# RWKV scans: one set of operand tiles for all products of a step, pairwise products on halves of the rows, and the inverses' last transposes moved behind the state

## The chip, the cores and the metric

The kernel runs on one core of a Trainium2 chip. The metric is the device time of one execution in microseconds (us). The core's engines run their own instruction queues in order and wait for each other by semaphores: TensorE (PE; its weight loads are shown apart as PEld), VectorE (DVE), ScalarE (ACT), GpSimd (POOL), and SyncE (SP), which here issues DMA transfers.

## The reference, cut to what matters

One encoder layer on 1024 tokens of width 1024: windowed attention, a bidirectional RWKV-7 time mixing, gates, then an MLP and a gated embedding. The change touches the RWKV scan, one forward and one backward over 8 heads of 64:

```python
def step(state, inp):
    r_t, w_t, k_t, v_t, a_t, b_t = inp
    sa = jnp.einsum('dbhij,dbhj->dbhi', state, a_t)
    state = (state * w_t[..., None, :] + sa[..., :, None] * b_t[..., None, :]
             + v_t[..., :, None] * k_t[..., None, :])
    y = jnp.einsum('dbhij,dbhj->dbhi', state, r_t)
    return state, y
...
y = ys[0] + jnp.flip(ys[1], axis=1)
```

## The kernel before

The kernel computes the scan in 16 steps of 64 tokens (s = 0 to 15), both directions d = 0, 1 in each step. Earlier it has written, per direction and chunk, two operands to DRAM: `ra_d` (for each of four head pairs j a [128 rows, 128 columns] block; rows are the two heads' 64 channels, columns the 64 tokens of a and the 64 of r, already decayed inside the chunk) and `bk_d` (the same layout for b and k). From them a step makes

- the pairwise products of all tokens of a chunk (`products`, into PSUM tiles `gps`, masked by VectorE into `gm`). One full-array matmul makes both heads of a pair: the stationary operand is `bkp` with both heads' rows, and the moving one is `rm`, a tile in which the other head's rows are zero. `rm` and `bkp` are loaded for `products` alone, one step ahead;
- the chunk's keys transposed (`operands`, tile `tm`, from another copy of bk, `bkc`), and ra scaled on ScalarE by the decay of the chunk before (`rac`, a second copy of ra, loaded by `load_step` at the start of the step before it is used);
- w (`wps`, copied to `Wt`), u (`ups`: the chunk's inverse `zi` times `Wt`, copied into `UV`), the state's addition (`sps`, then `Tc`, the state `Sb` and its decayed copy `Sc`), and the output (`yps`, into `y`).

The inverse of a chunk's triangular matrix is taken for four chunks at once, once every four steps: `low` products (`lps`, copied to `lt` and `Lc`), then on VectorE a transpose `Lp`, 62 small multiplies and adds into `Z` (`tmp`, `Z`), and two transposes `Zn` and `Zt` of 1024 columns; `end_inverse` makes the off-diagonal blocks with TensorE (`qps`) at the end of the fourth step.

TensorE's order in the scan is written out by hand: `gap(i)` puts `FILL[i]` filler matmuls (gates `gmm`, then the attention's up-projection `uaps`) between the stages of a step. The helper `mmo` (its matmuls all show line L209) keeps that order. The other engines' order and SP's come from the scheduler, by priority. PSUM tiles named `gps`, `tmps`, `lps`, `qps` and `mups` share two buffers.

Of the kernel before, what the change touches and what calls it, by code (L numbers as in the profile page):

```python
# [17 lines left out]
P = 128  # L18
# [120 lines left out]
def block_kernel(ctx: ExitStack, tc: tile.TileContext, I: dict, out: bass.AP):  # L139
# [638 lines left out]
    def inverse(pl, lt):  # L778

        Lc = pl.tile([P, 32, 32], F32, name="Lc", tag="inv", bufs=3)  # L780
        for r0 in range(0, P, 32):
            k = r0 // 32 % 2
            nc.scalar.copy(Lc[r0:r0 + 32], lt[r0:r0 + 32, :, 32 * k:32 * k + 32])
        Lp = pl.tile([P, 32, 32], F32, name="Lp", tag="inv", bufs=3)
        nc.vector.transpose(out=Lp, in_=Lc.rearrange("s p t -> s t p"))
        Z = pl.tile([P, 32, 32], F32, name="Z", tag="inv", bufs=3)
        nc.gpsimd.memset(Z, 0.0)
        nc.gpsimd.memset(Z.rearrange("p r c -> p (r c)")[:, ::33], 1.0)
        tmp = pl.tile([P, 256], F32, name="tmp", bufs=1)
        for t in range(31):  # L790
            n, m = 31 - t, t + 1
            tv = tmp[:, 0:n * m].rearrange("p (n m) -> p n m", m=m)
            nc.vector.tensor_tensor(
                out=tv, in0=Lp[:, t + 1:32, t:t + 1].broadcast_to([P, n, m]),
                in1=Z[:, t:t + 1, 0:m].broadcast_to([P, n, m]), op=ALU.mult)
            nc.vector.tensor_tensor(out=Z[:, t + 1:32, 0:m], in0=Z[:, t + 1:32, 0:m], in1=tv, op=ALU.add)
        Zn = pl.tile([P, 32, 32], F32, name="Zn", tag="inv", bufs=3)
        Zt = pl.tile([P, 32, 32], F32, name="Zt", tag="inv", bufs=3)
        nc.vector.transpose(out=Zn.rearrange("r p c -> r c p"), in_=Z.rearrange("p r c -> p c r"))
        nc.vector.transpose(out=Zt.rearrange("c p r -> c r p"), in_=Z)  # L800
        return Zn, Zt
# [32 lines left out]
    rms = [BP.tile([P, 2, NP, P], F32, name=f"rm{i}") for i in range(2)]  # L834
    for t_ in rms:
        nc.gpsimd.memset(t_, 0.0)
    prods = {}

    def load_products(s, d):

        c = chunk(s, d)
        for q in range(2):
            nc.sync.dma_start(rms[d][own[q], q], ra_d[d, c][own[q]])
        b_ = BP.tile([P, NP, P], F32, name="bkp", bufs=2)
        nc.sync.dma_start(b_, bk_d[d, c])
        prods[s, d] = b_

    lts, zzs, lows = {}, {}, {}
    with ExitStack() as s2:
# [16 lines left out]
        for n in range(NT):  # L866
# [49 lines left out]
            if n == LOW_AT:  # L916
                lts[0] = list(low0)[-1]
                for d in range(ND):
                    load_products(0, d)
            if n == INV_AT:  # L920
                zzs[0] = inverse(BI, lts[0])
# [144 lines left out]
    ch_ra, ch_bk, ch_tm, ch_uv, Sc = {}, {}, {}, {}, {}  # L1066
# [4 lines left out]
    def products(s, d):  # L1071

        b_ = prods.pop((s, d))
        for h in range(2):
            ps = ps_gps([P, 2, 2, P], "gps")
            for j in range(2):
                mmo(ps[:, j], b_[:, 2 * h + j, :], rms[d][:, :, 2 * h + j, :], start=True, stop=True)
            nc.vector.tensor_tensor(  # L1078
                out=gm[d][:, s % NB, 4 * h:4 * h + 4, :], in0=ps.rearrange("p j q t -> p (j q) t"),
                in1=gmask[:, d, :].unsqueeze(1).broadcast_to([P, 4, P]), op=ALU.mult)  # L1080
        if s + 1 < NCH:
            load_products(s + 1, d)

    def load_step(s):

        UV = B.tile([P, ND, NH, 64], F32, name="UV", bufs=2)
        for d in range(ND):
            c = chunk(s, d)
            b_ = B.tile([P, NP, P], F32, name="bkc", bufs=2)
            nc.sync.dma_start(b_, bk_d[d, c])  # L1090
            r_ = B.tile([P, NP, P], F32, name="rac", bufs=4)
            nc.sync.dma_start(r_, ra_d[d, c])
            nc.sync.dma_start(UV[oth[d], d], v_d[c * C:(c + 1) * C, :].rearrange("t (h i) -> t h i", i=64))
            nc.gpsimd.memset(UV[own[d], d], 0.0)
            ch_ra[s, d], ch_bk[s, d] = r_, b_
        ch_uv[s] = UV

    def operands(s):

        for d in range(ND):  # L1100
            tp = ps_gps([P, NP, P], "tmps")
            for q in range(NP):
                tc.keep_in_program_order(nc.tensor.transpose(tp[:, q, :], ch_bk[s, d][:, q, :], ident))
            t_ = B.tile([P, NH, 64], F32, name="tm", bufs=4)
            nc.scalar.copy(t_, tp.rearrange("p q (h j) -> p (q h) j", h=2))  # L1105
            ch_tm[s, d] = t_
        for d in range(ND):
            if s > 0:
                for j in range(NP):
                    r_ = ch_ra[s, d][:, j, :]  # L1110
                    nc.scalar.activation(out=r_, in_=r_, func=AF.Copy, scale=Dt[:, d, j, s - 1:s])
# [11 lines left out]
    def wb_part(s, wp):  # L1123

        if s > 0:
            for q in range(NP):
                for d in range(ND):
                    mmo(wp[own[d], 2 * q:2 * q + 2, :], ch_ra[s, d][:, q, 0:64], Sb[1 - s % 2][:, d, q, :, :],
                        start=False, stop=True, skip_group_check=True)
# [3 lines left out]
    def u_part(s):  # L1133
# [6 lines left out]
        nc.scalar.copy(UV[own[1], 1], up[own[1]])  # L1140

    def s_part(s):
# [11 lines left out]
        if s < NCH - 2:  # L1154
            Sc[s] = B.tile([P, ND, NP, 64], F32, name="Sc")
            nc.vector.tensor_tensor(out=Sc[s], in0=Tc, in1=Dt[:, :, :, s].unsqueeze(3).broadcast_to([P, ND, NP, 64]), op=ALU.mult)

    def y_part(s):
        yp = PB.tile([P, ND, NP, C], F32, name="yps", bufs=1)
        for d in range(ND):  # L1160
            for q in range(NP):
                os = [yp[own[e], d, q, :] for e in range(2)]
                if s > 0:
                    for e in range(2):
                        mmo(os[e], Sb[1 - s % 2][:, d, q, e, :], ch_ra[s, d][:, q, 64:128], start=True, stop=False)
# [22 lines left out]
    load_step(0)  # L1188
# [19 lines left out]
    for s in range(NCH):  # L1208
# [23 lines left out]
        if nxt:  # L1232
            load_step(s + 1)
# [4 lines left out]
        gap(2)  # L1238
        if more:
# [5 lines left out]
        y_part(s)  # L1245
        wp = wa_part(s + 1) if nxt else None
# [613 lines left out]
```

## Time and profile before

| | |
|---|---|
| median of three runs | 1809.24 us (1803.22 to 1815.18) |
| profiled execution | 1803.17 us |
| its span, first to last instruction | 1801.4 us |
| mean granted TensorE clock | 0.983 |
| TensorE busy | 1702.8 us, 95% |
| VectorE busy | 1147.4 us, 64% |
| ScalarE busy | 882.0 us, 49% |
| products in the scan | first at 511 us, last at 832 us |

The busy share is an average over stages with different limits. A row of a timeline gives the start, the duration, the engine, the line, the operation, the output and inputs, and in square brackets the idle time before it with what ended that. Durations of matmuls overlap, so how long a stage holds TensorE is read from the starts of what stands ahead of it and behind it. float32 matmuls show two records each.

### The profile page before, as it was taken

What the parts mean: (1) busy time and instruction counts of PE and PEld (TensorE: products, weight loads), DVE (VectorE), ACT (ScalarE), POOL (GpSimd) and SP (SyncE); (2) the same over time, 40 slices, a digit from 0 to 9 for tenths busy, and PEclk for the clock granted to TensorE, in tenths of its full rate; (3) what the DMA queues carried; (4) which work ended last, traced back from release to release, by engine and by line L of the source; (5) the groups of instructions that cost most, each with busy time, mean ns of one, the idle gap of its engine ahead of it and who ended that gap; (6) DMA issues with size and microseconds to landing.
All of it is one profiled execution on the core that took longest, in us unless ns stands there. A gap on an engine that the chain in (4) does not pass through costs nothing. (4 is left out here: it accounts for less than half of the span.)

```text
span 1801.4 us, 29643 instructions
## 1 busy us (share of the span) xinstructions
PE 1702.8 (95%) x11288; PEld 1367.5 (76%) x11288; DVE 1147.4 (64%) x1955; ACT 882.0 (49%) x1624; POOL 279.0 (15%) x241
## 2 busy tenths in 40 slices
PE   7999998899999898989889989999999999999998
PEld 7987675666677777867568867888888888888887
DVE  5667887345936556676564387767666877685432
ACT  5546775357754555456632255444444444554221
POOL 3343223331232121111232000000000000000000
PEclk9999999999999999999999999999999999999999
DMA  5353446574377474576565305454456983674111
GB/s 199 96 136 120 145 144 198 159 198 116 102 205 204 132 201 142 172 204 206 176 218 179 106 36 164 158 164 141 150 166 224 324 258 114 191 222 134 60 41 47
DMA packets 281998, 285.96 MB, mean 159 GB/s; under 512 B 49408, under 2 KB 195712, under 8 KB 281728
## 3 DMA queue, kind: packets, MB, share of 16 engines
q1 hardware_dynamic: 273600, 270.76, 48.9%
q0 software_dynamic: 7824, 12.59, 2.5%
q8 instruction: 89, 1.46, 0.3%
q10 hardware_dynamic: 432, 0.73, 0.1%
q14 instruction: 53, 0.43, 0.1%
HBM read 203.26 MB, written 80.74 MB: 158 GB/s over the span
## 5 line engine op out<-in xcount | busy, mean ns | idle before, releaser
L1742 PE MATMUL ff2ps<-th,sl 128*128 128x512 f32 x448 | 174.3, 389 | 0.0
L1742 PE MATMUL ff2ps<-tl,sh 128*128 128x512 f32 x448 | 174.3, 389 | 0.0
L1742 PE MATMUL ff2ps<-th,sh 128*128 128x512 f32 x448 | 173.9, 389 | 0.0
L189 POOL TENSOR_TENSOR wlo<-wst,whi 128x512 fp32r<-128x512 f32 x76 | 104.6, 1389 | 269.2 <-ACT whi L188 223.6
L176 POOL TENSOR_TENSOR rstd<-ms,neghalf 128x1 f32<-128x1 f32 x24 | 13.2, 552 | 791.3 <-DVE ms L174 791.3
L188 ACT CAST sh<-sst 128x512 fp32r<-128x512 f32 x109 | 67.7, 622 | 99.9 <-PE ff2ps L1742 51.3
L189 DVE TENSOR_TENSOR sl<-sst,sh 128x512 fp32r<-128x512 f32 x109 | 75.0, 688 | 47.5 <-ACT sh L188 47.3
L1742 PEld LDWEIGHTS ff2ps<-th,sh 128*128 128x128 f32 x448 | 84.0, 188 | 17.9 <-ACT th L188 0.3
L1742 PEld LDWEIGHTS ff2ps<-tl,sh 128*128 128x128 f32 x448 | 84.1, 188 | 17.6
L1742 PEld LDWEIGHTS ff2ps<-th,sl 128*128 128x128 f32 x448 | 84.1, 188 | 17.3
L188 ACT CAST whi<-wst 128x512 fp32r<-128x512 f32 x100 | 60.4, 617 | 60.8 <-DMA wst<-in_w_in_dram 22.9
L188 ACT CAST w1h<-w1st 128x512 fp32r<-128x512 f32 x48 | 28.4, 620 | 100.1 <-DMA w1st<-in_w_ff_dram 66.6
L189 DVE TENSOR_TENSOR w1l<-w1st,w1h 128x512 fp32r<-128x512 f32 x48 | 31.8, 687 | 54.5 <-ACT w1h L188 54.5
L209 PE MATMUL gps<-rm,bkp 128*128 128x256 f32 x256 | 62.4, 386 | 1.6 <-ACT tm L1105 0.9
L1078 DVE TENSOR_TENSOR gm<-gps,gmask 128x512 f32<-128x512 f32 x64 | 43.8, 688 | 29.6 <-PE gps L209 29.6
L219 PE MATMUL mm<-hh,wlo 128*128 128x512 f32 x144 | 58.4, 406 | 2.5 <-DVE wlo L189 2.5
L215 PE MATMUL gmm<-hh,whi 128*128 128x512 f32 x144 | 58.9, 409 | 1.6 <-ACT whi L188 1.4
L219 PE MATMUL gmm<-hh,wlo 128*128 128x512 f32 x144 | 59.3, 412 | 1.1 <-POOL wlo L189 1.1
L215 PE MATMUL mm<-hh,whi 128*128 128x512 f32 x144 | 58.6, 407 | 1.7 <-ACT whi L188 1.7
L217 PE MATMUL gmm<-hl,whi 128*128 128x512 f32 x144 | 58.7, 408 | 0.0
L217 PE MATMUL mm<-hl,whi 128*128 128x512 f32 x144 | 57.9, 402 | 0.0
L209 PEld LDWEIGHTS gps<-rm,bkp 128*128 128x128 f32 x256 | 47.2, 189 | 11.3 <-ACT tm L1105 2.1
(410 smaller groups left out, 4975.2 us busy)
## 6 DMA issues: line engine op xcount, KB each, us to landing
wst<-in_w_in_dram SPq DMA_DIRECT2D x92, 256.0 KB, 3.6
tst<-in_w_ff_dram SPq DMA_DIRECT2D x80, 256.0 KB, 3.9
w1st<-in_w_ff_dram SPq DMA_DIRECT2D x32, 512.0 KB, 5.4
hid_S<-h SPq DMA_DIRECT2D x64, 256.0 KB, 2.1
sst<-hid_S SPq DMA_DIRECT2D x64, 256.0 KB, 3.1
hid_A<-h SPq DMA_DIRECT2D x48, 256.0 KB, 2.0
sst<-hid_A SPq DMA_DIRECT2D x45, 256.0 KB, 3.5
ra_d<-ra SPq DMA_DIRECT2D x8, 1024.0 KB, 4.6
```

The lines of the kernel that those rows point to most:

```text
L176: nc.gpsimd.tensor_tensor(out=r, in0=ms, in1=neghalf.broadcast_to([P, width]), op=ALU.pow)
L188: a = nc.scalar.copy(hi, src)
L189: b = (lo_eng or nc.vector).tensor_tensor(out=lo, in0=src, in1=hi.bitcast(F32), op=ALU.subtract)
L209: tc.keep_in_program_order(nc.tensor.matmul(*a, **kw))
L215: mm(ps, ah, bh, start=(i == 0), stop=False)
L217: mm(ps, ah, bl, start=False, stop=False)
L219: mm(ps, al, bh, start=False, stop=(i == n - 1))
L1078: nc.vector.tensor_tensor(out=gm[d][:, s % NB, 4 * h:4 * h + 4, :], in0=ps.rearrange("p j q t -> p (j q) t"), in1=gmask[:, d, :].unsqueeze ...
L1742: nc.tensor.matmul(banks[bs][i], x_[:, isl], y_, start=fresh and p + j == 0, stop=p == NPR - 1 and j == 2, skip_group_check=True)
```

## The change

1. `products` takes row halves. For each head pair it issues two matmuls, one per head, on 64 rows each (rows 0 to 63 and 64 to 127), with 128 stationary and 128 moving columns, each into a PSUM tile of its own. The zero-padded `rm` tiles and their memsets go. Each of the two masks on VectorE comes after all eight matmuls.
2. ra and bk are loaded once per step and direction into tiles that products, transposes and state products share: four rotating tiles for ra, three for bk. The loads of step s + 1 are issued behind `products(s)`, which is called two steps ahead of use. Steps 1 and 2 are loaded at the start. `load_step` becomes `load_v`, which loads only v.
3. The scaling of ra on ScalarE (`decayed`) is called after `u_part` of the step before, not with the transposes.
4. The inverse's two last transposes (`inverse_turned`) are called behind `y_part` of the fourth step and held on VectorE behind the last operation of the state (`Sc`).

```diff
+    def inverse_turned(pl, Z, behind=None):
         Zn = pl.tile([P, 32, 32], F32, name="Zn", tag="inv", bufs=3)
         Zt = pl.tile([P, 32, 32], F32, name="Zt", tag="inv", bufs=3)
-        nc.vector.transpose(out=Zn.rearrange("r p c -> r c p"), in_=Z.rearrange("p r c -> p c r"))
-        nc.vector.transpose(out=Zt.rearrange("c p r -> c r p"), in_=Z)
+        a = nc.vector.transpose(out=Zn.rearrange("r p c -> r c p"), in_=Z.rearrange("p r c -> p c r"))
+        b = nc.vector.transpose(out=Zt.rearrange("c p r -> c r p"), in_=Z)
+        if behind:
+            after(a, behind)
+            after(b, a)
         return Zn, Zt
...
+    NRA, NBK = 4, 3
+    def load_ra(s, d):
+        nc.sync.dma_start(ra_t[s % NRA, d], ra_d[d, chunk(s, d)])
+    def load_bk(s, d):
+        nc.sync.dma_start(bk_t[s % NBK, d], bk_d[d, chunk(s, d)])
...
     def products(s, d):
-        b_ = prods.pop((s, d))
-        for h in range(2):
-            ps = ps_gps([P, 2, 2, P], "gps")
-            for j in range(2):
-                mmo(ps[:, j], b_[:, 2 * h + j, :], rms[d][:, :, 2 * h + j, :], start=True, stop=True)
+        b_, r_ = bk_t[s % NBK, d], ra_t[s % NRA, d]
+        pss = [ps_gps([P, NP, P], "gps") for _ in range(2)]
+        for j in range(NP):
+            for q in range(2):
+                mmo(pss[q][:, j], b_[own[q], j, :], r_[own[q], j, :], start=True, stop=True)
+        for q in range(2):
             nc.vector.tensor_tensor(
-                out=gm[d][:, s % NB, 4 * h:4 * h + 4, :], in0=ps.rearrange("p j q t -> p (j q) t"),
-                in1=gmask[:, d, :].unsqueeze(1).broadcast_to([P, 4, P]), op=ALU.mult)
-        if s + 1 < NCH:
-            load_products(s + 1, d)
+                out=gm[d][:, s % NB, q::2, :], in0=pss[q],
+                in1=gmask[:, d, :].unsqueeze(1).broadcast_to([P, NP, P]), op=ALU.mult)
+        if 1 < s < NCH - 1:
+            load_ra(s + 1, d)
+            load_bk(s + 1, d)
...
         u_part(s)
         gap(2)
+        if nxt:
+            decayed(s + 1)
...
         y_part(s)
+        if s % NB == NB - 1 and s // NB < 3:
+            b = s // NB + 1
+            zzs[b] = inverse_turned(BI, zzs[b], state[0])
```

VectorE at the end of the first inverse that runs inside the scan (step 3). Before, from the last operations of the chain on:

```order
L793 TENSOR_TENSOR tmp<-Lp,Z 128x31
L796 TENSOR_TENSOR Z<-Z,tmp 128x31
L799 STREAM_TRANSPOSE Zn<-Z 128x32x32
L800 STREAM_TRANSPOSE Zt<-Z 128x32x32
L1139 COPY UV<-ups 64x512
L1078 TENSOR_TENSOR gm_4655<-gps,gmask 128x512 x2
L1150 TENSOR_TENSOR Tc<-sps,Sc 128x512
L1153 COPY Sb_4657<-Tc 64x8x64
L1156 TENSOR_TENSOR Sc<-Tc,Dt 128x512
L1130 COPY Wt<-wps 64x512
```

The same place in the change, from the copy of UV on (the chain's last operations stand directly ahead of it):

```order
L1151 COPY UV<-ups 64x512
L1092 TENSOR_TENSOR gm_4653<-gps,gmask 128x4x128 x2
L1165 TENSOR_TENSOR Tc<-sps,Sc 128x512
L1168 COPY Sb_4655<-Tc 64x8x64
L1171 TENSOR_TENSOR Sc<-Tc,Dt 128x512
L803 STREAM_TRANSPOSE Zn<-Z 128x32x32
L804 STREAM_TRANSPOSE Zt<-Z 128x32x32
L1142 COPY Wt<-wps 64x512
```

The two transposes moved from ahead of UV to behind Sc, past the two masks and the three operations of the state.

ScalarE in steps 4 and 5, before:

```order
L773 COPY lt<-lps 128x4x64 x2
L1152 COPY Sb_4656<-Tc 64x8x64
L773 COPY lt<-lps 128x4x64 x2
L1111 ACTIVATE rac<-rac,Dt 128x128 x2
L1105 COPY tm<-tmps 128x512 x2
L1111 ACTIVATE rac<-rac,Dt 128x128 x6
L773 COPY lt<-lps 128x4x64 x2
L1131 COPY Wt<-wps 64x512
```

and in the change (`rac_4661` is the ra tile of a later step):

```order
L773 COPY lt<-lps 128x4x64 x2
L1167 COPY Sb_4654<-Tc 64x8x64
L773 COPY lt<-lps 128x4x64 x2
L1115 COPY tm<-tmps 128x512 x2
L773 COPY lt<-lps 128x4x64 x2
L1123 ACTIVATE rac_4661<-rac_4661,Dt 128x128
L1143 COPY Wt<-wps 64x512
L1123 ACTIVATE rac_4661<-rac_4661,Dt 128x128 x3
```

The eight scalings around the two copies tm are gone from there; those of the next step stand around the copy of Wt and, further on, behind that of UV.

ScalarE at the end of the first inverse inside the scan (step 3), between the copy of UV and the copies `Q` of the products that use Zn, before:

```order
L1140 COPY UV<-ups 64x512
L817 COPY zi<-Zt 32x32x32 x2
L1152 COPY Sb_4657<-Tc 64x8x64
L1172 COPY y<-yps 128x4x64 x2
L1111 ACTIVATE rac<-rac,Dt 128x128 x5
L1105 COPY tm<-tmps 128x512 x2
L1111 ACTIVATE rac<-rac,Dt 128x128 x3
L188 CAST whi<-wst 128x512
L312 ACTIVATE gth<-gmm 128x512
L814 COPY Q<-qps 32x512 x4
```

and in the change:

```order
L1152 COPY UV<-ups 64x512
L1123 ACTIVATE rac_3040<-rac_3040,Dt 128x128 x4
L1167 COPY Sb_4655<-Tc 64x8x64
L1187 COPY y<-yps 128x4x64 x2
L824 COPY zi<-Zn 32x32x32 x2
L824 COPY zi<-Zt 32x32x32
L1115 COPY tm<-tmps 128x512 x2
L824 COPY zi<-Zt 32x32x32
L312 ACTIVATE gth<-gmm 128x512
L821 COPY Q<-qps 32x512 x4
```

The two copies from Zn stood ahead of UV before, and all four copies into zi now stand between y and Q, three of them ahead of the copies tm. On TensorE only the products differ: where four matmuls of 128x256 stood between two fillers, eight of 128x128 stand now.

60 lines of the change are left out of this document (30 added, 30 removed).

## The prediction

> **What bounds the kernel now.** The page's busy table comes first, then a table of the scan by stretches (start and end in us; then for TensorE, its weight loads, VectorE, ScalarE and GpSimd the busy time and, in brackets, the count; then granted clock, DMA share, GB/s).
>
> ```profile
> PE 1702.8 (95%) x11288; PEld 1367.5 (76%) x11288; DVE 1147.4 (64%) x1955; ACT 882.0 (49%) x1624; POOL 279.0 (15%) x241
> ```
>
> ```profile
> 511.40:563.90 52.50, 49.77 (x749) 40.55 (x747) 15.16 (x23) 27.03 (x56) 9.50 (x9) 1.00 0.79 210
> 563.90:606.20 42.30, 36.11 (x457) 29.59 (x456) 40.30 (x83) 18.37 (x41) 10.13 (x11) 1.00 0.69 193
> 606.20:656.60 50.40, 47.56 (x848) 39.44 (x848) 13.53 (x21) 29.03 (x60) 8.11 (x9) 0.94 0.54 150
> 656.60:698.80 42.20, 35.92 (x457) 29.59 (x456) 40.18 (x82) 18.19 (x40) 10.14 (x11) 0.99 0.68 192
> 698.80:745.00 46.20, 45.64 (x848) 38.06 (x848) 14.04 (x23) 28.23 (x57) 8.27 (x10) 0.97 0.48 139
> 745.00:790.80 45.80, 38.17 (x580) 31.31 (x579) 44.33 (x102) 19.94 (x44) 8.22 (x9) 0.99 0.73 202
> 790.80:880.00 89.20, 79.82 (x1099) 62.56 (x1100) 51.61 (x79) 54.07 (x98) 16.36 (x15) 0.96 0.64 190
> ```
>
> TensorE is 95% busy over the whole span, so time taken out of its queue shortens the kernel. The scan, from 511 to about 880 us, is not uniform. I cut it where an inverse begins and ends on VectorE. In the second, fourth and sixth row VectorE is busy 40.30 of 42.30, 40.18 of 42.20 and 44.33 of 45.80 us: there VectorE sets the pace and TensorE waits for it. In the other rows TensorE is the limit (49.77 of 52.50). A saving on TensorE counts in the one kind of stretch, a saving on VectorE in the other.
>
> **Inverses' transposes held back.** VectorE and TensorE at the end of the first inverse inside the scan, the same wait one round later, and for comparison a wait in the step before (start, duration, instruction, idle time before it and what ended that):
>
> ```profile
> 601.83 2.07 DVE L799 STREAM_TRANSPOSE Zn<-Z 128x1024 f32<-128x1024 f32 x1
> 603.80 1.88 DVE L800 STREAM_TRANSPOSE Zt<-Z 128x1024 f32<-128x1024 f32 x1
> 605.52 0.65 DVE L1139 COPY UV<-ups 64x512 f32<-64x512 f32 x1
> ...
> 606.23 1.98 PE L209 MATMUL sps<-UV,tm 128*64 128x64 f32 x32 [4.05 <-DVE UV L1139]
> ...
> 698.82 0.48 PE L209 MATMUL sps<-UV,tm 128*64 128x64 f32 x4 [4.04 <-DVE UV L1139]
> ...
> 583.56 1.35 PE L209 MATMUL sps<-UV,tm 128*64 128x64 f32 x32 [1.17 <-DVE UV L1139]
> ```
>
> The state products (sps) wait 4.05 us for the copy of UV, and VectorE ran both transposes just ahead of that copy. With them behind it, UV starts at 601.83 in place of 605.52 and sps 3.69 us earlier, at 602.54. Nearly all of the wait goes; TensorE had been idle from 606.23 - 4.05 = 602.18, so VectorE's own chain stays late by about 0.4. What the hold-back puts at risk is the user of Zn, the products qps that end the inverse:
>
> ```profile
> 609.50 0.69 DVE L1156 TENSOR_TENSOR Sc<-Tc,Dt 128x512 f32<-128x512 f32 x1
> 623.32 0.68 DVE L1130 COPY Wt<-wps 64x512 f32<-64x512 f32 x1 [13.12 <-PE wps L209]
> ...
> 603.99 2.09 ACT L817 COPY zi<-Zn 32x1024 f32<-32x1024 f32 x2 [4.78 <-DVE Zn L799]
> 642.26 1.05 ACT L1105 COPY tm<-tmps 128x512 f32<-128x512 f32 x2
> ...
> 615.85 0.34 PE L209 MATMUL qps<-Zn,lt 32*32 32x32 f32 x10 [0.43 <-ACT tm L1105]
> ...
> 606.00:609.50 3.50, 3.27 (x64) 0.53 0.00 0
> ```
>
> After the 4 us wait the granted clock was 0.53 until 609.5: 3.27 us of work that full speed does in 1.7, a loss of 1.5 (the same 32 sps took 1.98 us here and 1.35 after the short wait). Before, qps was ready 615.85 - 0.43 - 606.23 = 9.2 us after sps; without the slow clock 7.7. Now the path on the other side: Sc ended 3.96 us after sps, about 3.35 at full clock; Zn ends 2.07 later (5.4); ScalarE, in the new order, makes two copies from Zn (2.09), one from Zt (half of that) and only then the first tm copy (half of 1.05) that frees the PSUM buffer for qps: 9.1. So qps starts at 602.54 + 9.1 = 611.65 in place of 615.85, a gain of **4.2 us**, with a new wait of 1.4 inside it. Behind the held transposes VectorE has the copy of Wt, before which it idled 13.12 us: covered. Two rounds give **8.4**. The third inverse ends after its step's state is done, so holding back changes nothing there. Bounds: 3.7 less 1.4 (the clock not regained) to 3.7 plus 1.5 a round, 4.6 to 10.4.
>
> **Pairwise products on half rows.** Eight records (two for a float32 matmul) of the products now; eight records of transposes with 128 moving columns; products of 64x64 blocks on both row halves; a stage that changes the array's division, and the matmul after each:
>
> ```profile
> 511.37 1.89 PE L209 MATMUL gps<-rm,bkp 128*128 128x256 f32 x8
> 513.32 0.39 PE L209 MATMUL gmm<-hl,whi 128*128 128x512 f32 x1
> ...
> 516.67 1.03 PE L1103 MATMUL tmps<-ident,bkc 128*128 128x128 f32 x8
> 517.78 0.40 PE L209 MATMUL gmm<-hh,whi 128*128 128x512 f32 x1
> ...
> 542.73 0.27 PE L209 MATMUL lps<-la,lb 64*64 64x64 f32 x1
> 542.75 0.27 PE L209 MATMUL lps<-lb,la 64*64 64x64 f32 x1
> 542.84 0.22 PE L209 MATMUL lps<-la,lb 64*64 64x64 f32 x1
> ...
> 559.41 1.15 PE L209 MATMUL ups<-Wt,zi 128*64 128x64 f32 x32
> 560.83 0.40 PE L209 MATMUL gmm<-hl,whi 128*128 128x512 f32 x1
> ```
>
> Fillers follow each other every 0.23 us, so a product occupies 513.32 - 0.23 - 511.37 = 1.72 us, and the transposes 517.78 - 0.23 - 516.67 = 0.88, 0.11 a record. The new form has 16 records of 128 columns. Nothing in the trace has 64 rows by 128 columns; the bounds are 8 x 0.11 (both halves at once) and 16 x 0.11. The nearest row is lps: four records, on both row halves, start within 0.02 us, and the next four 0.1 later. I take the halves as running at once, 0.88. They add two changes of the array's division: ups has 32 records, 16 pairs at 0.058, 0.93, but holds TensorE for 560.83 - 0.23 - 559.41 = 1.19, and starts 0.09 late, so 0.35 a product. A product then takes 1.23 and saves **0.5**. [...]
>
> Where do the 32 products stand? The records of the old products by stretch (busy, count):
>
> ```profile
> 511.40:563.90 52.50, 15.29 (x64) 1.00 0.79 210
> 563.90:606.20 42.30, 7.77 (x32) 1.00 0.69 193
> ```
>
> ```profile
> 512.43 0.69 DVE L1078 TENSOR_TENSOR gm<-gps,gmask 128x512 f32<-128x512 f32 x1 [9.39 <-PE gps L209]
> ```
>
> Eight are in the first stretch, four in each other. The 12 in VectorE's stretches save nothing. Something is also given back: VectorE masked the first PSUM buffer while TensorE filled the second (512.43, 1.06 us after the start); now both are full only at the end, so the second is free about 1.4 + 2 x 0.69 = 2.8 us after a product's start, and TensorE, four fillers later, is back at 2.2. The four start-up products follow each other at that distance and give 0.9 together; three blocks' first low products lose 0.4 each, 1.2. The other 16 give 8.0, of which 1.0 goes because the last four run beside an epilogue that waits for other engines. Sum 0.9 + 8.0 - 1.2 - 1.0 = **6.7**. The mask's output is now in pieces of 128 elements, which no row shows alone; I leave it at 0.69 (each 0.1 us more would lengthen a VectorE stretch by 0.8). In VectorE's order the last mask of a round now stands behind Lp, the first transpose of the inverse; the work there is the same in sum.
>
> **Operands loaded once, and decayed earlier.** The scaling of ra on ScalarE (rac) waited for its transfer:
>
> ```profile
> 641.66 0.69 ACT L1111 ACTIVATE rac<-rac,Dt 128x128 f32<-128x128 f32 x2 [3.03 <-DMA rac<-ra_d]
> 642.87 0.33 PE L209 MATMUL lps<-la,lb 64*64 64x64 f32 x2 [2.22 <-ACT tm L1105]
> 643.00:646.00 3.00, 2.84 (x38) 0.57 0.92 262
> 816.45 0.69 ACT L1111 ACTIVATE rac<-rac,Dt 128x128 f32<-128x128 f32 x2 [1.46 <-DMA rac<-ra_d]
> 577.06 0.58 ACT L1131 COPY Wt<-wps 64x512 f32<-64x512 f32 x1 [2.22 <-DVE Wt L1130]
> ```
>
> ```profile
> PE lps L209 <- ACT tm L1105: 2.9, 4, 2.2
> PE tmps L1103 <- ACT lv L1030: 2.1, 1, 2.1
> ```
>
> The second fence is the list of waits (total, times, longest). At 641.66 rac had kept ScalarE 3.03 us, tm stood behind it, and TensorE waited 2.22 for tm; the clock then fell to 0.57 for 3 us, 1.3 more. The new loads are issued a step ahead, and rac leaves this place. I count the four waits of lps (2.9), the clock (1.3) and 1.5 of the 2.1 for lv (the 1.46 ahead of it): **5.7**; bounds 0 and 6.3. In its new place one activation stands ahead of a Wt copy and three ahead of UV's; ScalarE idled 2.22 us before that Wt copy, which hides it, and without that cover it is 0.39 a step. SP now puts six operand transfers ahead of the first UV instead of two; UV is first needed 12 us later, so nothing is lost.
>
> **Sum.** 8.4 + 6.7 + 5.7 = 20.8. The profiled execution took 1803.17 us around a span of 1801.4: 1782.4. The median of the runs shown is 1809.24, which would give 1788.4. I take 1785, between them.
>
> **Rivals.** *The gain is half.* Row halves overlap poorly, or ScalarE's copies of Zn push qps later than 9.1, or another transfer is late in rac's place: 4.6 + 4 + 3 = 11.6 off, 1792 to 1798. For it: behind the freed sps wait stands VectorE's chain, 0.4 us late, and behind qps stands ScalarE. Against it: three separate terms would have to shrink together. *The halves run one after another.* A product takes 16 x 0.11 + 0.35 = 2.11, 0.39 more on 20 products, plus 8; the rest gives 14.1: about 1797 to 1803. Against it stand the lps rows. *Slower: the weight loads of the two halves do not overlap.* Each weight load of gps takes 0.19:
>
> ```profile
> L209 PEld LDWEIGHTS gps<-rm,bkp x256: 186/190/193, 511.1 to 831.9; 128*128 128x128 f32 x128
> ```
>
> Sixteen in a row make 3.04 + 0.35 = 3.39 us a product, 1.67 more; over 32 products 53, of which VectorE's stretches hide some 10, and less the 14.1 above, 29 slower: 1832 to 1838. It decides against the change once a product takes more than about 2.4 us. Against it: the four lps, each with a load, start within 0.02 us.
>
> **Chances.** Forecast 0.60 (1768 to 1791), half gain 0.22, one after another 0.10, slower 0.08. The range 1768 to 1803 leaves out the slower case and the forecast's edges. About 1% is what a measurement of this kernel can tell from no change: faster by over 1% is below 1791, so 0.60; within it 0.32; slower 0.08.
>
> **What would show it.** Right: sps at each inverse's end waits under 1 us for UV and its 32 records take 1.35; a product spans about 1.2 us, with pairs of records 0.11 apart; no rac waits for a transfer. Wrong: qps waiting over 2 us for tm or Zn; gps records 0.11 or 0.19 apart one by one; VectorE's stretches longer than 38.6 us (42.3 less 3.7), which would mean that TensorE or the masks now hold up the inverse.

## The result and the profile after

| | before | after |
|---|---|---|
| median (4 runs each) | 1810.57 us (1803.22 to 1815.18) | 1786.46 us (1784.45 to 1795.6) |
| ratio, 95% interval | | 0.988 (0.9831 to 0.9929) |
| profiled execution, span | 1803.17, 1801.4 us | 1788.35, 1786.6 us |

A second comparison gave 1811.15 and 1789.61 us, ratio 0.9895 (0.9848 to 0.9942). The forecast was 1785. The two profiled executions differ by 14.8 us, not by 24: the one of before ran 7 us under its median, the one of after 2 us over its own. The page's engines and its main DMA queue (packets, MB), then the stretches of the scan, cut as before:

```profile
PE 1689.6 (95%) x11544; PEld 1353.2 (76%) x11544; DVE 1148.1 (64%) x1955; ACT 884.8 (50%) x1624; POOL 276.7 (15%) x239
...
q1 hardware_dynamic: 263872, 253.98, 45.8%
```

```profile
508.80:556.70 47.90, 46.84 (x813) 36.92 (x812) 13.84 (x21) 28.01 (x59) 9.71 (x10) 1.00 0.59 161
556.70:595.40 38.70, 34.09 (x490) 27.24 (x488) 36.99 (x81) 17.09 (x39) 9.98 (x10) 1.00 0.40 121
595.40:641.40 46.00, 44.76 (x880) 36.28 (x880) 16.11 (x21) 31.13 (x60) 8.20 (x10) 0.96 0.53 139
641.40:680.15 38.75, 34.03 (x491) 27.24 (x489) 37.02 (x81) 17.10 (x39) 9.98 (x10) 1.00 0.45 132
680.15:726.10 45.95, 44.63 (x879) 36.05 (x880) 16.83 (x23) 30.48 (x58) 8.20 (x10) 0.96 0.40 113
726.10:773.95 47.85, 38.05 (x613) 31.84 (x611) 46.74 (x102) 22.71 (x49) 9.23 (x10) 0.93 0.67 180
773.95:865.00 91.05, 82.57 (x1136) 64.10 (x1137) 51.06 (x79) 53.08 (x92) 15.15 (x14) 0.91 0.44 137
```

The first two inverses' stretches (rows two and four) went from 42.30 and 42.20 us to 38.70 and 38.75, and VectorE still fills them (36.99). The TensorE stretches (rows one, three, five) went from 52.50, 50.40 and 46.20 to 47.90, 46.00 and 45.95. Behind them nothing was gained: the third inverse's stretch grew from 45.80 to 47.85 us, and from its end to the last gps of the epilogue it takes 113.8 us where it took 113.3. Two things show there. The granted clock, the third column from the right, is 0.93 and 0.91 in the last two rows where it was 0.99 and 0.96. And in the third stretch VectorE itself has more to do, 46.74 us in place of 44.33: one mask more (0.7 us), and four of its instructions, in place of two, run 0.7 to 1.5 us longer than their like elsewhere. One of them, and one of its kind at its usual length:

```profile
750.65 1.16 DVE L796 TENSOR_TENSOR Z<-Z,tmp 128x247 f32<-128x247 f32 x1
753.74 0.39 DVE L796 TENSOR_TENSOR Z<-Z,tmp 128x240 f32<-128x240 f32 x1
```

In the first two stretches four such instructions stand in each, at the same places of the program, where the kernel before had five. What makes them long no run shows.

The stages that the prediction named, in the trace of after (timeline; state products, the inverse's off-diagonal blocks, and one product between fillers):

```profile
595.43 1.35 PE L209 MATMUL sps<-UV,tm 128*64 128x64 f32 x32 [0.61 <-DVE UV L1151]
604.55 2.29 PE L209 MATMUL qps<-Zn,lt 32*32 32x32 f32 x128 [1.12 <-ACT tm L1115]
...
680.15 1.35 PE L209 MATMUL sps<-UV,tm 128*64 128x64 f32 x32 [0.62 <-DVE UV L1151]
689.30 2.21 PE L209 MATMUL qps<-Zn,lt 32*32 32x32 f32 x128 [1.15 <-ACT tm L1115]
...
508.46 0.39 PE L219 MATMUL gmm<-hh,wlo 128*128 128x512 f32 x1
508.78 1.16 PE L209 MATMUL gps<-rac,bkc 64*128 64x128 f32 x16
509.87 0.50 PE L209 MATMUL gmm<-hh,whi 128*128 128x512 f32 x1
510.21 0.39 PE L209 MATMUL gmm<-hl,whi 128*128 128x512 f32 x1
```

The 4 us wait of sps is 0.61 and 0.62 us, qps starts 9.12 and 9.15 us behind sps, and a product holds TensorE from 508.46 + 0.23 = 508.69 to 510.21 - 0.23 = 509.98, 1.29 us in place of 1.72. What TensorE waits for from 505 to 900 us (total, times, longest), and what the scaling of ra on ScalarE waits for:

```profile
PE qps L209 <- DVE Zn L803: 6.4, 1, 6.4
PE sps L209 <- DVE UV L1151: 5.1, 5, 1.6
PE ups L209 <- DVE Wt L1142: 5.0, 5, 1.3
...
ACT rac L1123 <- PE gps L209: 24.9, 14, 2.8
```

No rac waits for a transfer of ra any more (25.1 us in 16 waits before); it waits for TensorE's products, and no matmul waits for it. The largest single wait of TensorE is now the one for Zn at the third inverse's end, 6.4 us (4.8 before).

### The profile page after: what moved, and what is told of

The parts are those of the page before. It is cut to its first block, busy times and chain, and to the rows that moved or that the text cites. A ratio compares the mean times of both kernels' runs of the same rounds, so it can differ in the third digit from the quotient of the medians.

```text
span 1786.6 us, 29998 instructions
## 1 busy us (share of the span) xinstructions
PE 1689.6 (95%) x11544; PEld 1353.2 (76%) x11544; DVE 1148.1 (64%) x1955; ACT 884.8 (50%) x1624; POOL 276.7 (15%) x239
## 3 DMA queue, kind: packets, MB, share of 16 engines
q1 hardware_dynamic: 263872, 253.98, 45.8%
## 5 line engine op out<-in xcount | busy, mean ns | idle before, releaser
L1123 ACT ACTIVATE rac<-rac,Dt 128x128 f32<-128x128 f32 x120 | 40.3, 393 | 27.0 <-PE gps L209 24.9
L189 DVE TENSOR_TENSOR w1l<-ssum,w1h 128x512 fp32r<-128x512 f32 x64 | 43.0, 687 | 16.1 <-ACT w1h L188 16.1
```

Of the source, the lines that this page charges most:

```text
L189: b = (lo_eng or nc.vector).tensor_tensor(out=lo, in0=src, in1=hi.bitcast(F32), op=ALU.subtract)
```

## How the runs are compared: the scan with and without the slow clock

The sum of the terms is not visible in one total, because the granted clock differs between executions of one kernel: 0.977 to 0.983 in the four of the second comparison (1800.23 and 1787.58 us). In the scan of after TensorE's granted clock falls to 0.5 for 3.41, 6.83 or 10.24 us at a time, in that of before for 3.41 or 6.83. In the trace of after such stretches between 600 and 910 us begin at 606.4, 691.8, 743.0, 770.4, 838.6, 859.0, 876.2, 893.2 and 906.8: the distances (85.4, 51.2, 27.4, 68.2, 20.4, 17.2, 17.0, 13.6) are all whole multiples of 3.41 us within 0.2, the step of the reading. Each 3.41 us at half clock costs 1.7; the losses in the table below are whole multiples of that, 7 to 13 times. With the scan cut into windows of 3.41 us on that grid, all 17 windows between 500 and 915 us in which TensorE was busy for under 1.6 us (traces of before, of after and of the hold-back alone; 0.00 to 1.59 us busy in the first two) were followed by a slow one; in the other eleven traces 61 of 64 were. Of the 49 windows of the three traces with 1.6 to 2.8 us only nine were: four of the five that held qps, whose blocks are 32x32, and five of the other 44. Three busier windows (2.8 to 3.4 us) were followed by a slow one too; they were slow themselves and held qps. The changed kernel was profiled a second time for this:

> The changed kernel once more. From the traces so far I read: of the time from the first product to the last gps<-sge, what is left after taking off the clock's loss (1 us slice by slice, 1 minus the granted clock) is 380.7 us before and 362.0 after, and the loss, in whole windows of 3.4 us at half clock (1.7 us each), 12 and 17 us. Theory (the full-clock time belongs to the kernel, the loss to how idle time falls on a window grid that is not tied to the kernel): the full-clock time repeats within 0.5 us, the loss comes out anywhere from 12 to 22 us and in other places. Rival (the loss belongs to the kernel too): the same windows at the same places.

The same place in both executions, one window and the next (columns as in the table of stretches):

```profile
603.01:606.42 3.41, 2.29 (x120) 1.87 (x120) 0.00 (x0) 3.36 (x5) 0.00 (x0) 1.00 0.39 142
606.42:609.83 3.41, 3.41 (x29) 2.76 (x24) 0.00 (x0) 3.31 (x7) 0.01 (x1) 0.52 0.22 82
```

```profile
603.29:606.70 3.41, 2.25 (x79) 1.74 (x79) 0.42 (x1) 3.36 (x5) 0.00 (x0) 1.00 0.58 161
606.70:610.12 3.42, 3.42 (x100) 2.75 (x94) 0.00 (x0) 3.30 (x7) 0.00 (x0) 1.00 0.21 77
```

The wait in it is 1.12 us in the one and 1.16 in the other; relative to the kernel the grid lies about 0.7 us earlier in the second (the window begins 6.9 us behind sps, 7.6 in the first), the window holds less of qps, and the next one runs at full clock.

The theory holds for the sums (361.9 and 362.3 us at full clock, 17.1 and 13.7 lost). Of the places it holds in part: the slow windows behind the first two qps are gone in the second execution, but those at the third inverse's end and near 839 and 876 us stand in both. So each trace is read twice: the scan's length, from the start of the first product to that of the last gps<-sge of the epilogue, and the same less the loss (1 minus the granted clock, summed over slices of 1 us). For before that is 904.06 - 511.37 = 392.69 less 11.9, for after 887.73 - 508.78 = 378.95 less 17.1:

```profile
511.37 1.89 PE L209 MATMUL gps<-rm,bkp 128*128 128x256 f32 x8
...
904.06 1.02 PE L209 MATMUL gps<-sge 128*128 128x512 f32 x2
```

```profile
887.73 1.02 PE L209 MATMUL gps<-sge 128*128 128x512 f32 x2
```

The kernel before was run beside every kernel; its medians lay between 1806.3 and 1811.2 us, and each ratio is to its own. The last column does not depend on which execution was profiled: it is the span times the mean granted clock of the whole program, averaged over all the executions of the comparison.

| kernel | median us | ratio to before (95%) | scan in the profile | lost to the clock | scan at full clock | whole program at full clock, mean |
|---|---|---|---|---|---|---|
| before | 1810.57 | | 392.7 | 11.9 | 380.7 | 1771.2 to 1771.4 |
| hold-back alone | 1802.68 | 0.9983 (0.9964 to 1.0002) | 389.8 | 15.4 | 374.4 | 1767.1 |
| half rows alone | 1805.07 | 0.9993 (0.9975 to 1.0012) | 396.5 | 22.2 | 374.3 | 1762.3 |
| after without hold-back | 1797.15 | 0.9953 (0.9934 to 0.9972) | 383.3 | 17.1 | 366.3 | 1758.6 |
| after, halves in turn | 1796.77 | 0.9949 (0.993 to 0.9969) | 388.5 | 22.2 | 366.3 | 1760.3 |
| after | 1786.46 | 0.988 (0.9831 to 0.9929) | 379.0 | 17.1 | 361.9 | 1753.4 |
| after, again | 1789.61 | 0.9895 (0.9848 to 0.9942) | 376.0 | 13.7 | 362.3 | 1755.9 |
| after, decay late | 1789.39 | 0.9916 (0.9882 to 0.9949) | 380.5 | 17.1 | 363.5 | 1752.1 |
| after, all loads twice | 1805.78 | 1.0002 (0.9982 to 1.0022) | 386.0 | 20.5 | 365.5 | 1762.7 |
| after, scan loads twice | 1798.95 | 0.9938 (0.9911 to 0.9964) | 387.3 | 22.2 | 365.1 | 1759.0 |
| after, small second loads | 1791.37 | 0.9912 (0.9894 to 0.9931) | 380.1 | 17.1 | 363.1 | 1756.3 |
| ScalarE's copies | 1788.46 | 0.991 (0.9883 to 0.9937) | 376.5 | 18.8 | 357.8 | 1751.6 |
| and tm first | 1788.7 | 0.9909 (0.9878 to 0.994) | 375.5 | 18.8 | 356.7 | 1748.8 |
| and fillers moved | 1776.48 | 0.9802 (0.977 to 0.9835) | 367.5 | 11.9 | 355.6 | 1747.9 |

The scan at full clock repeats within 0.4 us for the changed kernel, the loss does not (17.1 and 13.7). Outside the scan the clock does the same: ahead of the first product it is at 0.5 for 23.9 us in the trace of before and for 13.7 in that of after, and with the same order of TensorE's instructions the first product starts anywhere from 508.8 to 514.1 us. The loss counts the idle part of a slow window too, and slow windows in stretches where VectorE sets the pace: in the third inverse's stretch of after it takes off 3.5 us though VectorE is busy 46.74 of 47.85. So the scan at full clock is good to about 1 us where the loss lies in like places, and to some 3 us where it does not. The last column gives the kernel before alike in all four comparisons that list its executions, and the changed kernel 2.5 us apart; differences smaller than that say nothing.

## Experiments

**The hold-back alone**, in the kernel before:

```diff
     zzs[b] = inverse(BI, lts[b])                     # now ends with Z
...
     y_part(s)
+    zzs[b] = inverse_turned(BI, zzs[b], state[0])    # at s = 3, 7, 11; behind Sc
```

> The kernel before with the held-back transposes alone. Theory (the wait of the state products goes, and the qps that end the inverse come 9.1 us after them): at both inverses' ends in the middle of the scan sps waits under 1 us for UV, its 32 records take 1.35 us, the first qps starts 9.1 us after sps, and from the first Lp of a round to the first qps it takes about 4.2 us less than before (51.95 us there). Sum 8.4 us: about 1802 if before is at 1810.5. Rival (the wait only moves from sps to qps, because Zn ends no earlier): Lp to qps stays at 51 to 52 us, sps to qps is over 11 us, and the time stays within 2 us of before.

Timeline of its first inverse's end:

```profile
601.07 1.35 PE L209 MATMUL sps<-UV,tm 128*64 128x64 f32 x32 [0.35 <-DVE UV L1146]
610.23 1.96 PE L209 MATMUL qps<-Zn,lt 32*32 32x32 f32 x112 [1.15 <-ACT tm L1112]
```

The steps are as predicted: sps waits 0.35, qps starts 9.16 behind it, and from Lp (562.38) to qps it is 47.85 us in place of 52.02. That is 4.2 us, and 3.5 in the next round. The rival (the wait only moves to qps) is out. But the total falls by 0.2% only, which the interval does not tell from nothing: the full-clock scan is 6.3 us shorter (the whole program 4.3 over all executions), and in the profile the clock takes 3.5 back. The slow windows behind the two sps are gone, but nine stand in the scan in place of seven, one of them behind the first qps.

**The half rows alone**, in the kernel before; its padded tiles are read on the rows that are not zero:

```diff
-            for j in range(2):
-                mmo(ps[:, j], b_[:, 2 * h + j, :], rms[d][:, :, 2 * h + j, :], start=True, stop=True)
+        for j in range(NP):
+            for q in range(2):
+                mmo(pss[q][:, j], b_[own[q], j, :], rms[d][own[q], q, j, :], start=True, stop=True)
...
```

The masks follow behind all eight matmuls, as in the changed kernel.

> The kernel before with the pairwise products on half rows alone; it reads the same padded tiles, and its loads are as before. Theory: a product holds TensorE 1.3 us in place of 1.72, only in the stretches where TensorE is the limit: 16 to 20 products, 6 to 8 us, about 1803 to 1805 if before is at 1810.5; VectorE's stretches stay at 42 us. [...] Rival 2 (most of the change's gain is here): 12 us or more.

Waits of TensorE, then the row of ScalarE's timeline behind the first of them:

```profile
PE tmps L1104 <- ACT lv L1030: 5.6, 1, 5.6
PE lps L209 <- ACT tm L1106: 4.5, 4, 2.8
```

```profile
816.19 0.69 ACT L1112 ACTIVATE rac<-rac,Dt 128x128 f32<-128x128 f32 x2 [4.95 <-DMA rac<-ra_d]
```

At full clock 6.4 us are gained in the scan, as forecast, and 9.1 in the whole program over all executions, but the total is the same as before: over those executions the clock's loss went from 32.8 to 40.9 us. With a shorter queue TensorE reaches the transfers' users earlier, and the transfers do not come earlier: tmps waits 5.6 us behind a rac that waited 4.95 for its transfer (2.1 and 1.46 before), lps 4.5 for tm (2.9 before). Such waits leave windows half empty, and 22.2 us of the profiled scan go to the clock; how much of that is due to these two waits was not tested apart.

**The changed kernel without the hold-back:**

```diff
-                    zzs[b] = inverse(BI, lts[b])
+                    zzs[b] = inverse_turned(BI, inverse(BI, lts[b]))
...
-            zzs[b] = inverse_turned(BI, zzs[b], state[0])
```

> The changed kernel with the transposes back right behind the inverse. Theory: 8.4 us slower than the changed kernel, about 1795 when that is at 1786.5; sps waits about 4 us for UV again at two inverses' ends, with the clock lowered behind it, and no wait of qps for tm. Rival (with TensorE's queue now shorter VectorE's chain is the path there anyway, and the hold-back only moves a wait): under 3 us slower, and qps then waits for Zn or UV by as much as sps did.

```profile
601.82 1.97 PE L209 MATMUL sps<-UV,tm 128*64 128x64 f32 x32 [4.26 <-DVE UV L1151]
```

1797.15 us where 1795 was expected: against 1789.61 and 1786.46, medians of other comparisons, the hold-back is worth 7.5 to 10.7 us here; at full clock 4.4 in the profiled scan, 2.7 to 5.2 over all executions. Set against half rows alone, in the same comparison, this kernel adds the loads: 7.9 us less in the medians. At full clock that is 8.0 in the two profiled scans, but 3.7 in the whole program over ten executions each; the other half is clock.

**The halves one after the other:**

```diff
-        for j in range(NP):
-            for q in range(2):
+        for q in range(2):
+            for j in range(NP):
                 mmo(pss[q][:, j], b_[own[q], j, :], r_[own[q], j, :], start=True, stop=True)
```

> The changed kernel with the products' matmuls in another order: the four of the lower half of the rows first, then the four of the upper half, the same matmuls otherwise. Theory (two records on different row halves run at once when they stand next to each other in the queue): now records follow each other at 0.11 us one by one, a product holds TensorE 16 x 0.11 + 0.35 = 2.1 us in place of 1.3, and 20 products outside VectorE's stretches cost 14 to 17 us: about 1800 to 1804 when the changed kernel is at 1786.5. Rival (a record on half the rows is cheaper by itself, or the queue finds the other half's records on its own): the product stays at 1.3 us and the time within 2 us of the changed kernel.

```profile
510.12 0.39 PE L219 MATMUL gmm<-hh,wlo 128*128 128x512 f32 x1
510.44 1.71 PE L209 MATMUL gps<-rac,bkc 64*128 64x128 f32 x16
512.08 0.50 PE L209 MATMUL gmm<-hh,whi 128*128 128x512 f32 x1
512.42 0.39 PE L209 MATMUL gmm<-hl,whi 128*128 128x512 f32 x1
```

The same 16 records take 1.71 us in place of 1.16, (1.71 - 0.27) / 15 = 0.096 apart against 0.059; the product holds TensorE 512.19 - 510.35 = 1.84 us, more than the padded full-array form (1.72). The kernel is 7 to 10 us slower (by the ratios 0.5 to 0.7%, 10 to 12 us), of which 4.4 in the profiled scan and 4.4 to 6.9 over all executions are at full clock. So the saving comes from neighbours on different row halves, not from smaller matmuls. The forecast of 14 to 17 us was too high: the step is 0.55 us rather than 0.8. That the first mask can run under the second half, which would give some back where products stand close together, was not measured apart.

**The scaling of ra at its old place, the loads early:**

```diff
             ch_tm[s, d] = t_
+        if s > 0:
+            decayed(s)
...
-        if nxt:
-            decayed(s + 1)
```

> The changed kernel with the scaling of ra (rac on ScalarE) back at its place of before, behind the operands' copies of tm; the loads stay a step ahead. Theory (what counts is that the transfers are issued a step ahead, the place only moves 8 activations of 0.33 us on ScalarE): rac waits for no transfer, the kernel is 0 to 3 us slower than the changed one (1786.5). Rival (the place counts): tm or the first wps<-Sb,rac of a step waits for ScalarE 1 to 2 us a step, and the kernel is 6 us slower or more.

1789.39 us, within the spread of the changed kernel's two medians; the scan at full clock is 363.5, 1.2 to 1.6 more, and the whole program over all executions is no longer at all (1752.1). No rac waits for a transfer. The place is worth little or nothing beside the loads.

**All operand loads a second time**, the second into tiles that nobody reads:

```diff
     def load_ra(s, d):
         nc.sync.dma_start(ra_t[s % NRA, d], ra_d[d, chunk(s, d)])
+        nc.sync.dma_start(BP.tile([P, NP, P], F32, name="dup", bufs=1), ra_d[d, chunk(s, d)])
...
```

and likewise half of bk behind `load_bk`.

> The changed kernel with a second copy of each operand load, into a tile that nobody reads (the whole of ra, half of bk): about three quarters of the traffic that was saved is back, at the early place. Theory (the time of issue counts, not the bytes): no wait of rac or tmps for a transfer, the time within 2 us of the changed kernel. Rival (the bytes count): lps, la or rac waits for DMA come back in the scan's transfer-heavy stretches, 5 us slower or more.

1805.78 us, all of the gain gone, but not for one cause: the scheduler put TensorE's instructions in the attention stage ahead of the scan in another order, and the first product started at 521.0 us in place of 508.8. Only the scan is comparable, 3.2 to 3.6 us longer at full clock. It was made again with the loads of the scan's steps alone, where TensorE's order is that of the changed kernel.

> The changed kernel with a second copy of the operand loads of steps 3 to 15 alone (the whole of ra, half of bk, into tiles that nobody reads); TensorE's order is that of the changed kernel throughout, which it was not in the run with all loads doubled. Theory (time of issue): full-clock time from the first product to the last gps<-sge within 1 us of 362.0, time within 3 us of the changed kernel. Rival (bytes): waits of lps or rac for transfers come back and the full-clock time is 4 us or more above.

**And once more with 16 floats a partition** in each second copy, which leaves SP's waits and takes the bytes away:

```diff
-    nc.sync.dma_start(B.tile([P, NP, P], F32, name="dup", bufs=1), ra_d[d, chunk(s + 1, d)])
+    nc.sync.dma_start(B.tile([P, 1, 16], F32, name="dup", bufs=1), ra_d[d, chunk(s + 1, d)][:, 0:1, 0:16])
...
```

> As the kernel with the scan's operand loads doubled, but each second copy is 16 floats a partition, 3% of the bytes and less; TensorE's order and the waits that each second copy carries on SP (for the copy before it into the same tile) stay. Theory A (SP's in-order queue was what the second copies hurt: with them the first la of block 1 was issued 35.4 us after the first product, in the changed kernel 29.7): la is late by 3 us or more again, lps waits for lb, and at least half of the 10 us that the doubled loads cost is still there, 1793 to 1799 when the changed kernel is at 1788. Theory B (bytes: landing times of the transfers grow with the traffic): la as early as in the changed kernel within 1.5 us, and the time within 2 us of it.

Waits of lps and of SP with full second copies, then with small ones, then the wait of SP in the kernel before:

```profile
PE lps L209 <- DMA lb<-bk_d: 3.5, 3, 2.2
SPq L1097 <- DMA dup<-ra_d: 32.5, 17, 4.5
```

```profile
PE lps L209 <- DMA lb<-bk_d: 1.9, 1, 1.9
SPq L1097 <- DMA dup<-ra_d: 17.2, 13, 3.1
```

```profile
SPq L843 <- PE gps L209: 58.1, 22, 5.5
```

The fillers' weight transfers (size, median us from issue to landing), with full copies and with small ones:

```profile
wst<-in_w_in_dram SPq DMA_DIRECT2D x26, 256.0 KB, 4.9
```

```profile
wst<-in_w_in_dram SPq DMA_DIRECT2D x26, 256.0 KB, 3.3
```

The full copies cost 9 to 12 us, the small ones 2 to 5; in the scan at full clock 2.8 to 3.2 and 0.8 to 1.2. The load la that the expectations speak of (block 1's second chunk, not its first) is issued 29.7 us behind the first product in the changed kernel, 35.4 with full copies, 32.5 with small ones, and 34.1 in the kernel before. So the loads behind a copy that waits for its tile come later as well: with the small copies, 16 floats a partition, SP waits 17.2 us for them (13 waits from 505 to 905) and la is issued 2.8 us later than in the changed kernel. Before, the loads of rm waited for the products that still read their one tile (58.1 us in 22 waits from 505 to 905). Neither theory holds alone: the small copies bring back half of la's delay and between a fifth and a half of the time, and with the bytes the transfers also land later (4.9 against 3.3 us). Nor did rac wait for a transfer with the full copies, as the rival had it; lps did. How queue and bytes divide the gain of the change itself was not measured.

**ScalarE makes VectorE's copies** of Wt and UV while VectorE makes an inverse:

```diff
-        nc.vector.tensor_copy(UV[own[0], 0], up[own[0]])
+        eng = nc.scalar.copy if s < NCH - NB and s % NB in (1, 2, 3) else nc.vector.tensor_copy
+        eng(UV[own[0], 0], up[own[0]])
```

Wt likewise, for s % NB in 2 and 3.

> The changed kernel, but while VectorE makes an inverse, the half of the Wt and UV copies that VectorE made is made by ScalarE, which makes the other half already and waits for VectorE's copy before it starts (5 copies of 0.67 us a round). Theory (VectorE sets the pace from Lp to sps): each of these stretches shrinks from 38.7 us to about 35.4, in three rounds 8 us less than the changed kernel, about 1778; ups and sps wait less for DVE. Rival 1 (ScalarE's queue is as late as VectorE's): waits of the same size with ScalarE as their end, no change. Rival 2 (TensorE's own work is the floor there, 34 us busy, or the clock falls in more windows): half of it, 1782.

```profile
PE gps L209 <- DVE gm L1092: 8.5, 7, 2.5
...
PE sps L209 <- ACT UV L1153: 0.8, 3, 0.3
```

A miss in time (1788.46), half in substance: TensorE waits no more for Wt, and 0.8 us for UV in place of 5.1, and at full clock the scan is 4.1 to 4.5 us shorter. But the stretches that were to shrink from 38.7 to 35.4 us, from Lp to sps, came out at 39.6 and 40.1. VectorE's lateness now shows at its masks (8.5 us, 0.8 in the changed kernel), and the clock takes the rest: two slow windows stand in the first of these stretches and one in the second, where after had none.

**And the copies of tm ahead of those of Zn** on ScalarE:

```diff
-            nc.scalar.copy(zi[r0:r0 + 32, :, 32 * k:32 * k + 32], src_[r0:r0 + 32])
+            z_ = nc.scalar.copy(zi[r0:r0 + 32, :, 32 * k:32 * k + 32], src_[r0:r0 + 32])
+            if last_tm[0] is not None:
+                after(z_, last_tm[0])
...
```

`last_tm[0]` is the last copy of tm.

> As the kernel with ScalarE's copies, and the copies of tm ahead of the copies of Zn on ScalarE at an inverse's end. Theory (qps waits 1.1 us for tm behind two copies of 1.05): that wait goes in two rounds, 2.2 us less than with ScalarE's copies alone, about 1776. Rival (qps then waits for Zn or for the transposes by as much): no difference to the kernel with ScalarE's copies.

```profile
598.17 1.15 PE L209 MATMUL sps<-UV,tm 128*64 128x64 f32 x32
605.90 2.21 PE L209 MATMUL qps<-Zn,lt 32*32 32x32 f32 x128
```

qps starts 605.90 - 598.17 = 7.73 us behind sps (8.93 with the copies alone) and waits for nothing: the step works and gives 1.2 us each time. The scan at full clock is 1.1 us shorter where 2.2 was forecast; the median (1788.7) does not show it.

**Fillers moved**, on top of both:

```diff
+FILLX = {0: (-2, -2, -1, -2, -1, -1, -2, 0), 1: (-2, 0, 0, 0, 0, 0, 0, 0),
+         2: (0, 0, 10, 0, 0, 0, 0, 0), 3: (0, 0, 3, 0, -1, -1, -2, -1)}   # by s % NB and gap
+FILLZ = 20                                                                # ahead of end_inverse(3)
...
+            fill(FILL[i] + (FILLX[s % NB][i] if s < 11 else 0) if more else FILLEND)
```

> The kernel with ScalarE's copies and tm first, and some 50 of the independent gate matmuls (0.23 us each) moved out of the stretches where TensorE is the limit to the places in VectorE's stretches where TensorE still waits: 10 ahead of the product that waits 2.45 us for a mask, 3 a step later, 20 ahead of the third inverse's qps (4.8 us for Zn). Theory (a stretch's time is set by the engine that is behind, so work of TensorE is free in VectorE's stretches and paid in the others): 49 x 0.23 = 11 us less at full clock than the kernel it is made from (356.8 from the first product to the last gps<-sge), fewer windows at half clock, about 1775 to 1780. Rival 1 (the fillers were the cover of other chains in the stretches they leave): new waits of ups, sps or qps there, under 4 us gained. Rival 2 (VectorE's stretches grow by what is put in): no gain.

```profile
511.48:879.02 367.54, 340.85 (x5360) 269.36 (x5359) 223.53 (x408) 226.94 (x435) 75.76 (x79) 0.97 0.51 149
```

```profile
PE gps L212 <- DVE gm L1099: 4.5, 2, 3.6
```

1776.48 us (1773.11 to 1779.15), ratio 0.9802: faster than both kernels (the changed one in the same comparison: 0.9895). The forecast of the time held; the one of its cause did not. At full clock the scan is 1.1 us shorter than without the move, not 11, and the whole program 0.9. The waits that were to be filled shrank: that of qps for Zn (4.8 us) is gone, and the products wait 4.5 us for masks where they waited 8.3. But others grew: the products wait 3.6 us for zi (1.9 without the move), and transposes and low products now wait 2.4 and 1.5 for masks. In its size that is rival 1, though mostly not with the matmuls that it named. Nearly all of the gain is the clock: 11.9 us lost in the profiled scan where 18.8 were, and over all executions 26.6 in the whole program where 38.4 were. That all four executions lie 8 us and more below all four of the kernel without the move speaks against luck; that the fuller windows are the cause was not tested apart.

## Why the prediction was right, step by step

- **The hold-back.** sps: under 1 us expected, 0.61 and 0.62 measured, 32 records in 1.35. qps behind sps: 9.1 expected, 9.12 and 9.15. Its new wait: 1.4 for tm expected, 1.12 and 1.15. VectorE's stretches: 38.6 expected, 38.7. Without its clock part the term was 8.4 - 2 x 1.5 = 5.4; measured in the scan at full clock 6.3 alone, 4.4 in the changed kernel (4.3 and 2.7 to 5.2 over all executions). The step that is not sure is "the clock regained": in the first profile of after a slow window stood again behind qps in both rounds, though the wait ahead was 1.1 us rather than 4; in the second profile in neither.
- **The half rows.** 1.23 us a product expected, 1.29 measured, so 0.43 saved (0.5 expected); 6.7 expected, 6.4 measured in the scan at full clock, 9.1 in the whole program over all executions. The halves run at once (0.059 a record; 0.096 in turn). The mask with pieces of 128 elements costs nothing more (683 ns in the median of 64, 691 before). What the sum left out is that this term had no value of its own in the kernel before: it came back as waits for transfers and as slow windows. It also put nothing for the third inverse, where the time from Lp to qps is 47.4 to 51.0 us in the kernels with half rows and VectorE's own copies, 45.8 and 46.2 without half rows.
- **The loads.** 5.7 expected (4.4 without the clock). Behind the half rows they bring 7.9 in the medians. The profiled scans put 8.0 of that at full clock, the ten executions of each kernel 3.7 and as much again to the clock; so the time was under-sized, and whether the term at full clock was stays open. The half rows had raised the waits that the loads remove (lps, tmps, gps for ScalarE: 2.9 + 2.1 + 1.4 before, 4.5 + 5.6 + 1.7 with half rows alone). The early place of the scaling, which the heading put beside the loads, is worth at most 1.2 to 1.6 of it. The loads alone, in the kernel before, were not run.
- **The sum.** At full clock 20.8 less 4.3 of clock is 16.5 forecast; measured are 18.4 to 18.8 in the profiled scans, 15.5 to 18.0 in the whole program over all executions. The clock was to give 4.3: in the profiled scans it took 1.8 to 5.2, over the executions of the second comparison the whole program's loss fell from 37.8 to 34.0. So the sum is right to about 2 us, and the clock's part is no property of the change. That the time came within 1.5 us is luck: the median of before moves by 5 us from comparison to comparison, and 1785 was chosen between the profiled execution and a median.
- **The rivals.** Row halves one after another: as an order of the queue it gives 1796.77, at the lower edge of its price; in the changed kernel it does not happen. Weight loads that do not overlap: a product's 16 loads would need 3.04 us by the prediction's row, and the whole product spans 1.16. Half the gain: the middle of the scan had the waits it named (VectorE behind UV, ScalarE behind qps), at the sizes in the sum. No run shows the 4 us that its sum leaves to the half rows; alone they gave 6.4 in the scan at full clock.

## What to carry to other kernels

The time that a part of a change saves need not show when the part is made alone: here the half rows gained 6 to 9 us at full clock and nothing in the time, while TensorE waited longer for late operands (tmps 5.6 us in place of 2.1, lps 4.5 in place of 2.9) and the clock took 8.1 us more of the whole program. So price the transfers against the new schedule, not the old one, and look at what the issuing queue stands behind. Read a stage's gain with the clock taken out, over more than one execution, and expect the clock to answer: in these traces a window of 3.4 us that a wait left less than half busy was followed by a slow one in 78 of 81 cases, and a slow one costs up to 1.7 us. Independent fillers where TensorE waits, with two edits on ScalarE that alone moved no median, gave a further 10 to 13 us here; what the move itself brought of that was nearly all clock.

## What was not expected of the hardware

- Of the 81 windows of 3.41 us in which TensorE was busy for under 1.6, 78 were followed by a slow one, partly busy ones (up to 1.59 us in the trace of after) as well as idle ones. A window with 2.29 us busy, most of it qps in 32x32 blocks, was followed by a slow one, and one with 2.25 was not; whether small blocks count for less was not tested.
- The loss in the scan ran from 11.9 to 22.2 us over these kernels, and 17.1 against 13.7 for the same one. The grid of the slow windows, counted from the program's start, lies from 0.0 to 3.1 us behind a multiple of 3.41 us in the fourteen traces (1.7 in that of before, 2.4 in that of after). That this makes the spread of the executions (1784.45 to 1795.6) would fit, but was not shown.
- Eight float32 matmuls on 64 rows each, alternating between the halves in the queue, hold TensorE 1.29 us, against 1.84 in turn and 1.72 for the four zero-padded full-array matmuls with twice the columns.
- VectorE instructions that run 0.7 to 1.5 us longer than others of their kind stand at fixed places of a program, four or five in each of the first two inverses' stretches before and after; their cause is open.
